# Eight start places modulo 128 bytes for the operands of a kernel's MLP products

## The chip, the core and the metric

The kernel runs on one core of a Trainium2 chip. A core has a matrix engine (TensorE, PE in the profile, with its loads of stationary operands shown apart as PEld), VectorE (DVE), ScalarE (ACT), GpSimd (POOL), and a queue that issues transfers (SyncE, SP). They work on tiles in an on-chip memory of 128 partitions; results of TensorE land in a second memory, PSUM. A tile takes the same bytes in every partition, so the place of an operand is one byte address, counted from the start of a partition.

The metric is the device time of one execution in microseconds (us), lower is better.

## The reference, cut to what matters

Two layers of a streaming encoder over 512 tokens of width 1024, in float32. A layer has a mixing part (a projection, pooling, differential attention, gated linear attention, an output projection) and an MLP; the change is in the MLP:

```python
def reference(x, ...):
    h = x
    for l in range(DEPTH):                    # 2
        u = rms_norm(h, norm1_g[l])
        ...                                   # the mixing part
        h = h + (mix @ w_out[l])
        z = rms_norm(h, norm2_g[l])
        h = h + jnp.square(jax.nn.relu(z @ w_mlp1[l])) @ w_mlp2[l]
    return rms_norm(h, final_norm_g)
```

`w_mlp1` is 1024 x 4096 and `w_mlp2` is 4096 x 1024 in each layer.

## The kernel before, in words

**Products in three.** Activations are kept transposed: a tile holds 128 features in the partitions and the 512 tokens along them. Each float32 operand is split into a high part in the type float32r and the float32r rest (`split`, L113 on: ScalarE casts the high part, L116; VectorE subtracts it, L117). A product is then three matmuls that add into one PSUM tile: high x high, high x low, low x high (`mm3`, L134 to L136, and `prod`, L904 to L906). The profile writes a matmul as out<-moving,stationary. The moving operand (activations, 512 or 256 columns) streams; the stationary operand (128 columns of weights) is loaded before it. For each matmul the trace has one load and one matmul.

**The first product of the MLP.** The 4096 features of the hidden layer are 32 output tiles of 128; two of them are a pair u, and four pairs are a quarter q, so there are 16 pairs in four quarters per layer. Pairs 0 and 1 of a layer are computed plainly (`plain`). The other 14 are computed by seven smaller products instead of eight (`seven`, a Strassen-like scheme over two halves of the input features and two halves of the tokens). The weights of a pair come in by DMA as raw1 and raw2; `prepare` makes four operands of them, each as a high and a low tile: a (tiles wh, wl), b, c and d (tiles bh, bl, ch, cl, dh, dl). On the moving side are the activations z (tiles zh, zl) and four sums of them, t1 to t4 (tiles th, tl), made once a layer (`sums_of_inputs`, `keep`). Each of the seven products is 12 matmuls of 256 columns:

| product, as the trace names it | moving | stationary |
|---|---|---|
| psx<-zh,wh | z | a |
| psz<-th,bh | t1 | b |
| psx<-th,ch | t2 | c |
| psy<-zh,dh | z | d |
| psz<-zh,ch | z | c |
| psx<-th,bh | t3 | b |
| psx<-th,wh | t4 | a |

That is 84 matmuls a pair, 28 pairs, 2352 matmuls.

**The second product.** The squared hidden tiles of a quarter are split into the tiles sh, sl (`acts`), which are the moving operand of the second product: for each of 8 output tiles m, one load of weights (`weights(wm2[l, q, m])`, tiles wh, wl), and 24 matmuls (8 tiles of the quarter x 3) into a PSUM tile psm (`second`). That is 1488 matmuls of 512 columns; the last two output tiles of the last quarter of layer 1 are done in token halves, which are 96 matmuls of 256 columns.

**Order.** TensorE's order in the MLP is that of the code. VectorE and ScalarE prepare the next pair's operands while TensorE works on this one (`prepare(u + 1)` stands behind `seven(u)`), so one pair's operands are ready ahead.

**Places.** A tile's address is given out by its pool when the program is built. All tiles named here begin at a multiple of 32 bytes. In the built program, modulo 128 bytes, zh, zl, wh and wl begin at 32, and th, tl, sh, sl and the b, c and d tiles begin at 96. Slices inside a tile step by multiples of 512 bytes, so they begin at the same place modulo 128 as their tile. Two places of the mixing part are read below: the tile y of the output projection (attention heads 2 and 3) begins at 0, and in the scores of the even heads the keys (kh, kl) begin at 0 and the queries (sq_) at 96.

Of the kernel before, what the change touches and what calls it, by code (L numbers as in the profile page):

```python
# [8 lines left out]
F32 = mybir.dt.float32  # L9
F32R = mybir.dt.float32r  # L10
# [23 lines left out]
PLAIN = 2  # L34
HT = T // 2
W = 16 + T
BIG = 1.0e30

LEAD = [(0, 0), (1, 0), (2, 0), (3, 0), (0, 1), (1, 1), (2, 1), (3, 1), (4, 0), (5, 0), (6, 0), (7, 0), (4, 1), (5, 1), (6, 1), (7, 1)]
# [30 lines left out]
def trunk(ctx: ExitStack, tc: tile.TileContext, xt, wfm, wdv, wgv, wout, wm1, wm2, poolw, wg2, par, con, msk, out, outt):  # L70
# [12 lines left out]
    def load(src, n=1024):  # L83
        raw = wp.tile([P, 1024], F32, name="raw", bufs=2)[:, 0:n]
        nc.sync.dma_start(out=raw, in_=src)
        return raw
# [33 lines left out]
            nc.vector.scalar_tensor_tensor(out=dst_l, in0=src, scalar=scale, in1=dst_h.bitcast(F32),  # L120
                                           op0=ALU.mult, op1=ALU.subtract)

    def cut(raw):
        n = raw.shape[1]
        wh = wp.tile([P, 1024], F32R, name="wh")[:, 0:n]
        wl = wp.tile([P, 1024], F32R, name="wl")[:, 0:n]
        split(wh, wl, raw)
        return wh, wl

    def weights(src, n=1024):  # L130
        return cut(load(src, n))

    def mm3(ps, sh, sl, mh, ml, first, last):
        nc.tensor.matmul(ps, sh, mh, start=first, stop=False)  # L134
# [98 lines left out]
    for l in range(L):  # L233
# [5 lines left out]
        for k in range(KT):  # L239
            for i, m, a, b in LOADS if l == 0 else ():  # L240
                if i == k:
                    if a == 0:
                        lead.append([wp.tile([P, 1024], F32R, name=n) for n in ("wh", "wl")])
                    split(lead[m][0][:, a:b], lead[m][1][:, a:b], first[m][:, a:b])
            split(uh[k], ul[k], h[k], g1[k])
        if l == 0:
# [558 lines left out]
        with ExitStack() as ph:  # L805
# [4 lines left out]
            sp = fast.enter_context(tc.tile_pool(name=f"sp{l}", bufs=1))  # L810
            acts, tz = {}, {}

            def plain(u, j):

                raw = wp.tile([P, 1024], F32, name="raw", bufs=2)
                nc.sync.dma_start(out=raw[:, 0:512], in_=wm1[l, u, j][:, 0:512])
                nc.sync.dma_start(out=raw[:, 512:1024], in_=wm1[l, u, 1 - j][:, 512:1024])
                wh, wl = cut(raw)
                ps = pm.tile([P, T], F32, name="psm", tag="pm")
                for k in range(KT):  # L820
                    s = slice(k * P, (k + 1) * P)
                    mm3(ps, wh[:, s], wl[:, s], zh[k], zl[k], k == 0, k == KT - 1)
                rl = mp.tile([P, T], F32, name="rl", bufs=3)
                nc.scalar.activation(rl, ps, AF.Relu)

                def rest():
                    nc.scalar.activation(rl, rl, AF.Square)
                    split(acts[u][0][:, j], acts[u][1][:, j], rl)

                return rest  # L830

            def sums_of_inputs():

                z = []

                def scaled_inputs(i):
                    zi = mp.tile([P, 2, T], F32R, name="z", tag=f"{'shsl'[2 * (i % 2):2 * (i % 2) + 2]}{2 + i // 2}", bufs=1).bitcast(F32)
                    for j in range(2):
                        nc.scalar.activation(zi[:, j], h[2 * i + j], AF.Copy, scale=g2[2 * i + j])
                    z.append(zi)  # L840

                def new(name):
                    return mp.tile([P, 4, HT], F32, name=name, tag="o4")

                def keep(i, t):
                    tz[i] = [sp.tile([P, 4, HT], F32R, name=f"t{n}{i}") for n in "hl"]
                    split(*tz[i], t)

                two = (slice(0, 2), slice(2, 4))
                t1 = new("t1")  # L850
                for i in range(2):
                    scaled_inputs(i)
                    nc.vector.tensor_sub(t1[:, two[i]], z[i][:, :, 0:HT], z[i][:, :, HT:T])
                keep(1, t1)
                t2 = new("t2")
                for i in range(2):
                    scaled_inputs(2 + i)
                    nc.vector.scalar_tensor_tensor(out=t2[:, two[i]], in0=t1[:, two[i]], scalar=-1.0, in1=z[2 + i][:, :, HT:T],
                                                   op0=ALU.mult, op1=ALU.subtract)
                keep(2, t2)  # L860
                yield
                t4 = new("t4")
                for i in range(2):
                    nc.vector.scalar_tensor_tensor(out=t4[:, two[i]], in0=t2[:, two[i]], scalar=-1.0, in1=z[2 + i][:, :, 0:HT],
                                                   op0=ALU.mult, op1=ALU.subtract)
                t3 = new("t3")
                for i in range(2):
                    nc.vector.tensor_sub(t3[:, two[i]], z[2 + i][:, :, HT:T], z[i][:, :, HT:T])
                keep(3, t3)
                keep(4, t4)  # L870

            def prepare(u):

                raw1 = load(wm1[l, u, 0])
                raw2 = sp.tile([P, 1024], F32, name="raw2", bufs=2)
                nc.sync.dma_start(out=raw2, in_=wm1[l, u, 1])
                a = cut(raw1)
                s13 = sp.tile([P, 2, 512], F32, name="s13")
                nc.vector.tensor_tensor(out=s13, in0=raw1.rearrange("p (a b) -> p a b", a=2),  # L879
                                        in1=raw2[:, 0:512].unsqueeze(1).broadcast_to([P, 2, 512]), op=ALU.add)  # L880
                b = [sp.tile([P, 2, 512], F32R, name=f"b{n}", bufs=2) for n in "hl"]
                split(*b, s13)
                s24 = sp.tile([P, 2, 512], F32, name="s24")
                nc.vector.tensor_add(s24[:, 0], s13[:, 1], raw1[:, 0:512])
                nc.vector.tensor_add(s24[:, 1], s24[:, 0], raw2[:, 512:1024])
                c = [sp.tile([P, 2, 512], F32R, name=f"c{n}") for n in "hl"]
                split(*c, s24)
                d = [sp.tile([P, 512], F32R, name=f"d{n}", bufs=2) for n in "hl"]
                split(*d, raw2[:, 512:1024])
                return a, b, c, d  # L890

# [65 lines left out]
            for q in range(QT):  # L957
                for u in range(q * UQ, (q + 1) * UQ):
                    if u == 0:
                        for i in range(PLAIN):  # L960
                            acts[i] = [mp.tile([P, 2, T], F32R, name=f"s{n}{i}", bufs=1) for n in "hl"]
                        left = [plain(0, 0)]
                        dg = token_norm(acc, True)[1]
                        left.append(plain(0, 1))
                        r2 = across(dg)
                        acc = sm.tile([P, T], F32, name="acc", bufs=1)
                        sums = sums_of_inputs()
                        next(sums)
                        left.append(plain(1, 0))
                        w = prepare(PLAIN)  # L970
                        left.pop(0)()
                        left.append(plain(1, 1))
                        list(sums)
                        for f in left:
                            f()
                    if u < PLAIN:
                        continue
                    acts[u] = [mp.tile([P, 2, T], F32R, name=f"s{n}{u % UQ}", bufs=1) for n in "hl"]
                    final = u % UQ == UQ - 1
                    old = late  # L980
                    late = seven(u, w, old, final)
                    if not final:
                        w = prepare(u + 1)
                    if old:
                        old[1]()
# [19 lines left out]
                every = slice(0, T)  # L1005
                lead = []
                for m in range(2):
                    w2t = weights(wm2[l, q, m])
                    ps = pm.tile([P, T], F32, name="psm", tag="pm")
                    second(ps, w2t, range(KT - 2), every)  # L1010
                    lead.append((ps, w2t))
                ends = l == L - 1 and q == QT - 1
                for m in range(KT - 2 if ends else KT):
                    if m < 2:
                        ps = lead[m][0]
                        second(*lead[m], range(KT - 2, KT), every)
                    else:
                        w2t = weights(wm2[l, q, m])
                        ps = pm.tile([P, T], F32, name="psm", tag="pm")
                        second(ps, w2t, range(KT), every)  # L1020
                    update(m, ps, every)
                    if q == QT - 1:
                        square_acc(acc, h[m], m == 0)
                    elif m == 2:
                        w = prepare((q + 1) * UQ)
                byhand.close()
                if ends:
                    w2t = [weights(wm2[l, q, m]) for m in range(KT - 2, KT)]
                    ph.enter_context(tc.manual_schedule(engines={mybir.EngineType.DVE}))
                    for half in range(2):  # L1030
                        n = slice(half * HT, (half + 1) * HT)
# [90 lines left out]
```

## Time and profile before

| | before |
|---|---|
| median of 2 runs | 1107.13 us (1106.85 to 1107.41) |
| the profiled execution | 1107.54 us, of which the trace's span is 1105.7 us |
| PE busy | 1090.8 us (99%), 6454 matmuls |
| DVE, ACT busy | 746.7 us (68%), 577.6 us (52%) |
| granted TensorE clock | 0.998 over the span |

Busy time of PE is the sum of intervals that overlap: matmuls are pipelined, and the next one starts before the one ahead has ended. How fast a row of matmuls goes is therefore read from the starts: the start of a later one less the start of an earlier one, divided by the number of matmuls between. This is called the pace below.

### The profile page before, as it was taken

How to read it: one execution, taken by the hardware profiler on the slowest of the kernel's cores; microseconds unless marked ns; L12 is line 12 of the kernel's file. 1: busy time of each engine (PE TensorE's matmuls, PEld its weight loads, DVE VectorE, ACT ScalarE, POOL GpSimd, SP SyncE). 2: the span in 40 equal slices, each digit the busy share in tenths (PEclk: the TensorE clock that was granted, in tenths of full speed). 3: DMA queues.
4: the chain of work that ended last, by engine and by line, in shares of the span. 5: the costliest groups of instructions: out<-in, count | busy, mean ns of one | idle time of the engine just before them, and what ended most of it. 6: DMA issues, size and time to landing. Idle time of an engine off the chain costs nothing.

```text
span 1105.7 us, 16213 instructions
## 1 busy us (share of the span) xinstructions
PE 1090.8 (99%) x6454; PEld 960.3 (87%) x6454; DVE 746.7 (68%) x1115; ACT 577.6 (52%) x998; POOL 47.4 (4%) x84
## 2 busy tenths in 40 slices
PE   7999999999999999999999999999999999999997
PEld 5888898888898898898887988888989989989986
DVE  5577774896676676675647588749766666666654
ACT  5526774685265264265434377748633733733742
POOL 2101000000000000000021100000000000000000
PEclk9999999999999999999999999999999999999999
DMA  6222211433322322312322131214232332332222
GB/s 210 86 65 71 77 58 57 146 104 108 120 96 88 122 97 84 124 60 68 103 61 84 59 95 58 79 56 152 96 115 86 106 115 81 111 114 79 75 76 76
DMA packets 32223, 102.75 MB, mean 93 GB/s; under 512 B 3698, under 2 KB 5524, under 8 KB 32148
## 3 DMA queue, kind: packets, MB, share of 16 engines
q1 hardware_dynamic: 31716, 101.17, 28.5%
q8 instruction: 50, 0.82, 0.3%
q10 hardware_dynamic: 432, 0.55, 0.1%
q14 instruction: 25, 0.20, 0.1%
HBM read 99.61 MB, written 2.10 MB: 92 GB/s over the span
## 4 chain that ended last, share of the span: by engine, by line
PE 97%; issue 1%; ACT 1%; DVE 1%; DMA 0%; SPq 0%; POOLq 0%; POOL 0%; DVEq 0%
PE psm L136 18%; PE psm L135 18%; PE psm L134 18%; PE psx L904 5%; PE psx L906 5%; PE psx L905 5%; PE psz L906 2%; PE psz L904 2%; PE psz L905 2%; PE psm L340 2%; PE psm L341 2%; PE psm L342 2%; PE po L483 1%; PE psy L904 1%; PE psy L906 1%; PE psy L905 1%
## 5 line engine op out<-in xcount | busy, mean ns | idle before, releaser
L116 ACT CAST wh<-raw 128x1024 fp32r<-128x1024 f32 (+2 forms) x155 | 160.0, 1034 | 293.9 <-PE psm L135 213.0
L117 DVE TENSOR_TENSOR wl<-raw,wh 128x1024 fp32r<-128x1024 f32 (+2 forms) x155 | 185.9, 1202 | 74.3 <-ACT wh L116 74.0
L136 PE MATMUL psm<-sh,wl 128*128 128x512 f32 (+1 forms) x528 | 204.5, 387 | 0.0
L135 PE MATMUL psm<-sl,wh 128*128 128x512 f32 (+1 forms) x528 | 203.3, 385 | 0.0
L134 PE MATMUL psm<-sh,wh 128*128 128x512 f32 (+1 forms) x528 | 201.5, 382 | 0.0
L1002 DVE TENSOR_TENSOR tm<-psm,rb 128x512 f32<-128x512 f32 (+1 forms) x66 | 44.5, 674 | 113.2 <-PE psm L136 113.2
L135 PEld LDWEIGHTS psm<-sl,wh 128*128 128x128 f32 x528 | 99.1, 188 | 21.5
L134 PEld LDWEIGHTS psm<-sh,wh 128*128 128x128 f32 x528 | 99.1, 188 | 20.6
L136 PEld LDWEIGHTS psm<-sh,wl 128*128 128x128 f32 x528 | 99.3, 188 | 18.5
L134 PE MATMUL psm<-uh,wh 128*128 128x512 f32 x224 | 95.7, 427 | 5.9 <-ACT uh L119 5.9
L135 PE MATMUL psm<-ul,wh 128*128 128x512 f32 x224 | 89.7, 400 | 0.5 <-DVE ul L120 0.5
L136 PE MATMUL psm<-uh,wl 128*128 128x512 f32 x224 | 89.5, 399 | 0.1
L134 PEld LDWEIGHTS psm<-uh,wh 128*128 128x128 f32 x224 | 43.1, 192 | 15.7 <-ACT uh L119 7.3
L340 PE MATMUL psm<-wh,uh 128*128 128x256 f32 (+1 forms) x192 | 56.6, 295 | 0.0
L342 PE MATMUL psm<-wh,ul 128*128 128x256 f32 (+1 forms) x192 | 54.7, 285 | 0.0
L341 PE MATMUL psm<-wl,uh 128*128 128x256 f32 (+1 forms) x192 | 54.6, 284 | 0.0
L135 PEld LDWEIGHTS psm<-ul,wh 128*128 128x128 f32 x224 | 43.1, 192 | 10.4 <-DVE ul L120 2.3
L136 PEld LDWEIGHTS psm<-uh,wl 128*128 128x128 f32 x224 | 43.0, 192 | 10.4 <-DVE wl L117 1.0
L453 ACT ACTIVATE pp<-psc,mn,nrt 128x128 f32<-128x128 f32 (+3 forms) x64 | 39.0, 615 | 13.9 <-DVE mn L450 12.0
L1003 DVE TENSOR_TENSOR h<-h,tm 128x512 f32<-128x512 f32 (+1 forms) x66 | 44.5, 674 | 1.5
L117 DVE TENSOR_TENSOR sl<-o,sh 128x1024 fp32r<-128x1024 f32 (+1 forms) x36 | 35.0, 987 | 11.2 <-ACT sh L116 11.2
L879 DVE TENSOR_TENSOR s<-raw,raw 128x1024 f32<-128x1024 f32 x28 | 34.2, 1221 | 6.4 <-DMA raw<-in_wm 6.4
(379 smaller groups left out, 2719.4 us busy)
## 6 DMA issues: line engine op xcount, KB each, us to landing
raw<-in_wm SPq DMA_DIRECT2D x120, 512.0 KB, 3.6
raw<-in_wfm SPq DMA_DIRECT2D x27, 512.0 KB, 3.6
raw<-in_wout SPq DMA_DIRECT2D x16, 512.0 KB, 3.6
raw<-in_wdv SPq DMA_DIRECT2D x8, 512.0 KB, 3.5
raw<-in_wm SPq DMA_DIRECT2D x16, 256.0 KB, 3.2
h<-in_xt SPq DMA_DIRECT2D x8, 256.0 KB, 6.2
raw<-in_wgv SPq DMA_DIRECT2D x4, 408.0 KB, 3.4
out<-o SPq DMA_DIRECT2D x8, 128.0 KB, 1.8
```

Source lines behind the costliest of these rows:

```text
L116: nc.scalar.copy(out=dst_h, in_=src)
L117: nc.vector.tensor_sub(dst_l, src, dst_h.bitcast(F32))
L134: nc.tensor.matmul(ps, sh, mh, start=first, stop=False)
L135: nc.tensor.matmul(ps, sh, ml, start=False, stop=False)
L136: nc.tensor.matmul(ps, sl, mh, start=False, stop=last)
L340: nc.tensor.matmul(ps, uh[k][:, ts], wh[:, s], start=k == 0, stop=False)
L341: nc.tensor.matmul(ps, uh[k][:, ts], wl[:, s], start=False, stop=False)
L342: nc.tensor.matmul(ps, ul[k][:, ts], wh[:, s], start=False, stop=k == KT - 1)
L904: nc.tensor.matmul(ps, sh[:, s], mh, start=first and k == 0, stop=False, skip_group_check=True)
L905: nc.tensor.matmul(ps, sh[:, s], ml, start=False, stop=False, skip_group_check=True)
L906: nc.tensor.matmul(ps, sl[:, s], mh, start=False, stop=k == 3, skip_group_check=True)
L1002: nc.vector.tensor_tensor(out=tm, in0=ps, in1=r2[:, n], op=ALU.mult)
```

## The change: what it does, and the diff

Tiles that hold operands of the MLP's products get 28 more floats (112 bytes) of room, and the operand begins at an offset inside the tile. The offsets are the eight entries of SPOT, in floats; in bytes they are 0, 32, 64, 96, 16, 48, 80, 112.

- The stationary operands a, b, c, d of pair u begin SPOT[u % 8] into their tiles.
- The stationary operands of the second product begin SPOT[m] into theirs, by output tile m.
- The moving operand of the second product, the tiles sh, sl of layer l and quarter q, begin SPOT[4 l + q] into theirs.
- The sums t1 to t4 begin 4 l floats into theirs: 0 bytes in layer 0, 16 in layer 1.
- The activations z and the weights of the plain pairs begin where they did.

The wider tiles shift the addresses of the tiles behind them; each tile still begins at the same place modulo 128 as before. The tiles now end at byte 229,072 of a partition, before at 224,992. The instructions of all five engines are the same, in the same order and with the same waits: only addresses differ, and no instruction is added or removed.

With "distance" for the start of the moving operand less the start of the stationary operand of the same matmul, modulo 128 bytes, the built programs have these numbers of matmuls:

| distance, bytes | 0 | 16 | 32 | 48 | 64 | 80 | 96 | 112 |
|---|---|---|---|---|---|---|---|---|
| seven products, before | 1344 | 0 | 0 | 0 | 1008 | 0 | 0 | 0 |
| seven products, after | 276 | 300 | 276 | 324 | 276 | 324 | 276 | 300 |
| second product (512 columns), before | 0 | 0 | 0 | 0 | 1488 | 0 | 0 | 0 |
| second product (512 columns), after | 192 | 192 | 192 | 192 | 168 | 192 | 168 | 192 |
| second product (256 columns), before | 0 | 0 | 0 | 0 | 96 | 0 | 0 | 0 |
| second product (256 columns), after | 0 | 0 | 0 | 0 | 48 | 0 | 48 | 0 |

The diff, cut to its core:

```diff
+PAD = 28
+SPOT = (0, 8, 16, 24, 4, 12, 20, 28)
...
-    def cut(raw):
+    def cut(raw, at=0):
         n = raw.shape[1]
-        wh = wp.tile([P, 1024], F32R, name="wh")[:, 0:n]
-        wl = wp.tile([P, 1024], F32R, name="wl")[:, 0:n]
+        wh = wp.tile([P, 1024 + PAD], F32R, name="wh")[:, at:at + n]
+        wl = wp.tile([P, 1024 + PAD], F32R, name="wl")[:, at:at + n]
...
-    def weights(src, n=1024):
-        return cut(load(src, n))
+    def weights(src, n=1024, at=0):
+        return cut(load(src, n), at)
...
+            def place(u):
+
+                at = SPOT[4 * l + u // UQ]
+                return [mp.tile([P, 2 * T + PAD], F32R, name=f"s{n}{u % UQ}", bufs=1)[:, at:at + 2 * T].rearrange("p (j n) -> p j n", j=2)
+                        for n in "hl"]
...
-                    tz[i] = [sp.tile([P, 4, HT], F32R, name=f"t{n}{i}") for n in "hl"]
+                    tz[i] = [sp.tile([P, 4 * HT + PAD], F32R, name=f"t{n}{i}")[:, 4 * l:4 * l + 4 * HT].rearrange("p (k n) -> p k n", k=4) for n in "hl"]
...
-                a = cut(raw1)
+                at = SPOT[u % 8]
+                a = cut(raw1, at)
...
-                b = [sp.tile([P, 2, 512], F32R, name=f"b{n}", bufs=2) for n in "hl"]
+                b = [sp.tile([P, 1024 + PAD], F32R, name=f"b{n}", bufs=2)[:, at:at + 1024].rearrange("p (a n) -> p a n", a=2) for n in "hl"]
...
-                    acts[u] = [mp.tile([P, 2, T], F32R, name=f"s{n}{u % UQ}", bufs=1) for n in "hl"]
+                    acts[u] = place(u)
...
-                    w2t = weights(wm2[l, q, m])
+                    w2t = weights(wm2[l, q, m], at=SPOT[m])
```

The tiles of c and d get the same treatment as those of b.

## Rows read from the trace of the kernel before

**Rows 1.** The page: busy time by engine, the granted clock, the chain.

```profile
span 1105.7 us, 16213 instructions
...
PE 1090.8 (99%) x6454; PEld 960.3 (87%) x6454; DVE 746.7 (68%) x1115; ACT 577.6 (52%) x998; POOL 47.4 (4%) x84
...
PEclk9999999999999999999999999999999999999999
...
PE 97%; issue 1%; ACT 1%; DVE 1%; DMA 0%; SPq 0%; POOLq 0%; POOL 0%; DVEq 0%
```

**Rows 2.** Waits, whole span: who waited for whom, us in total, times, longest.

```profile
ACT wh L116 <- PE psm L135: 213.0, 70, 6.2
...
DVE tm L1002 <- PE psm L136: 113.2, 47, 5.1
```

**Rows 3.** Groups by shape: count, busy us, mean ns, idle before.

```profile
L136 PE MATMUL psm<-sh,wl 128*128 128x512 f32 x496 | 195.4, 394 | 0.0
...
L904 PE MATMUL psx<-th,ch 128*128 128x256 f32 x112 | 31.7, 283 | 0.0
...
L904 PE MATMUL psx<-th,wh 128*128 128x256 f32 x112 | 30.9, 276 | 0.0
```

**Rows 4.** Timeline, PE, one round of seven products: start us, duration us, instruction.

```profile
480.72 0.28 PE L904 MATMUL psx<-th,wh 128*128 128x256 f32 x1
...
482.08 0.28 PE L904 MATMUL psx<-th,ch 128*128 128x256 f32 x1
...
483.52 0.29 PE L904 MATMUL psy<-zh,dh 128*128 128x256 f32 x1
...
484.90 0.28 PE L904 MATMUL psz<-zh,ch 128*128 128x256 f32 x1
...
486.26 0.28 PE L904 MATMUL psx<-th,bh 128*128 128x256 f32 x1
...
487.68 0.28 PE L904 MATMUL psx<-zh,wh 128*128 128x256 f32 x1
...
489.10 0.28 PE L904 MATMUL psz<-th,bh 128*128 128x256 f32 x1
...
490.53 0.28 PE L904 MATMUL psx<-th,wh 128*128 128x256 f32 x1
```

**Rows 5.** Timeline, PE, second product: the first of 24 matmuls, and of the next.

```profile
435.76 0.39 PE L134 MATMUL psm<-sh,wh 128*128 128x512 f32 x1
...
441.25 0.39 PE L134 MATMUL psm<-sh,wh 128*128 128x512 f32 x1
```

**Rows 6.** Timeline, PE, a plain product: matmuls 1, 13, 22 and 24 of 24.

```profile
215.40 0.39 PE L134 MATMUL psm<-zh,wh 128*128 128x512 f32 x1
...
218.16 0.39 PE L134 MATMUL psm<-zh,wh 128*128 128x512 f32 x1
...
220.20 0.39 PE L134 MATMUL psm<-zh,wh 128*128 128x512 f32 x1
...
220.65 0.39 PE L136 MATMUL psm<-zh,wl 128*128 128x512 f32 x1
```

**Rows 7.** Timeline, PE, output projection: six matmuls, and the next one.

```profile
187.25 0.39 PE L134 MATMUL psm<-y,wh 128*128 128x512 f32 x1
...
188.65 0.40 PE L134 MATMUL psx<-y,wxA 128*128 128x512 f32 x1
```

**Rows 8.** Timeline, PE, attention scores: the second of four matmuls, and the next product.

```profile
134.69 0.28 PE L446 MATMUL psc<-kl,sq__1084 128*128 128x256 f32 x1
...
135.04 0.39 PE L134 MATMUL psm<-uh,wh 128*128 128x512 f32 x1
```

**Rows 9.** Busy us (instructions) of PE, PEld, DVE, ACT, POOL, 480 to 490.

```profile
480.00:490.00 10.00, 10.00 (x88) 10.00 (x87) 8.57 (x12) 7.77 (x12) 0.00 (x0) 1.00 0.18 55
```

**Rows 10.** Groups by shape, DVE: count, busy us, mean ns, idle before.

```profile
L117 DVE TENSOR_TENSOR wl<-raw,wh 128x1024 fp32r<-128x1024 f32 x147 | 179.1, 1220 | 64.7 <-ACT wh L116 64.4
...
L1003 DVE TENSOR_TENSOR h<-h,tm 128x512 f32<-128x512 f32 x62 | 42.8, 690 | 1.4
...
L117 DVE TENSOR_TENSOR sl<-o,sh 128x1024 fp32r<-128x1024 f32 x20 | 24.5, 1226 | 5.7 <-ACT sh L116 5.7
...
L117 DVE TENSOR_TENSOR dl<-raw,dh 128x512 fp32r<-128x512 f32 x28 | 19.2, 686 | 0.3
...
L536 DVE TENSOR_TENSOR pl<-pl 128x512 f32<-128x512 f32 x8 | 5.5, 689 | 0.3
```

More of the change, by code (lines that the diff above doesn't have):

```diff
@@ L242, in trunk @@
                     if a == 0:
-                        lead.append([wp.tile([P, 1024], F32R, name=n) for n in ("wh", "wl")])
+                        lead.append([wp.tile([P, 1024 + PAD], F32R, name=n)[:, 0:1024] for n in ("wh", "wl")])
                     split(lead[m][0][:, a:b], lead[m][1][:, a:b], first[m][:, a:b])
@@ L836, in scaled_inputs @@
                 def scaled_inputs(i):
-                    zi = mp.tile([P, 2, T], F32R, name="z", tag=f"{'shsl'[2 * (i % 2):2 * (i % 2) + 2]}{2 + i // 2}", bufs=1).bitcast(F32)
+                    zi = mp.tile([P, 2 * T + PAD], F32R, name="z", tag=f"{'shsl'[2 * (i % 2):2 * (i % 2) + 2]}{2 + i // 2}",
+                                 bufs=1)[:, 0:2 * T].bitcast(F32).rearrange("p (j n) -> p j n", j=2)
                     for j in range(2):
@@ L885, in prepare @@
                 nc.vector.tensor_add(s24[:, 1], s24[:, 0], raw2[:, 512:1024])
-                c = [sp.tile([P, 2, 512], F32R, name=f"c{n}") for n in "hl"]
+                c = [sp.tile([P, 1024 + PAD], F32R, name=f"c{n}")[:, at:at + 1024].rearrange("p (a n) -> p a n", a=2) for n in "hl"]
                 split(*c, s24)
-                d = [sp.tile([P, 512], F32R, name=f"d{n}", bufs=2) for n in "hl"]
+                d = [sp.tile([P, 512 + PAD], F32R, name=f"d{n}", bufs=2)[:, at:at + 512] for n in "hl"]
                 split(*d, raw2[:, 512:1024])
@@ L960, in trunk @@
                         for i in range(PLAIN):
-                            acts[i] = [mp.tile([P, 2, T], F32R, name=f"s{n}{i}", bufs=1) for n in "hl"]
+                            acts[i] = place(i)
                         left = [plain(0, 0)]
@@ L1017, in trunk @@
                     else:
-                        w2t = weights(wm2[l, q, m])
+                        w2t = weights(wm2[l, q, m], at=SPOT[m])
                         ps = pm.tile([P, T], F32, name="psm", tag="pm")
@@ L1027, in trunk @@
                 if ends:
-                    w2t = [weights(wm2[l, q, m]) for m in range(KT - 2, KT)]
+                    w2t = [weights(wm2[l, q, m], at=SPOT[m]) for m in range(KT - 2, KT)]
                     ph.enter_context(tc.manual_schedule(engines={mybir.EngineType.DVE}))
```

## The prediction

> **What bounds the kernel now.** I read the page first. TensorE is busy 99% of the span, its clock is full in every slice, and the chain that ended last is PE for 97% [rows 1]. So only two things move the time: how fast TensorE gets through its matmuls, and whether somebody makes it wait. The view of waits, next, shows the feeders waiting for TensorE and not the other way round: ScalarE's casts of weights waited 213 us for buffers that TensorE still read, VectorE's updates 113 us for sums [rows 2]. In the groups by shape PE has no idle time ahead of the matmuls of the MLP, and products of the same size differ there: 283 ns a matmul for psx<-th,ch, 276 for psx<-th,wh [rows 3]. Busy times overlap, so I took the pace from starts in the timeline.
>
> One round of the seven products shows it [rows 4]. From one first matmul to the next, divided by 12:
>
> - distance 0 (moving and stationary operand begin at the same place modulo 128): psx<-th,ch 1.44 us, 120.0 ns a matmul; psx<-th,bh and psx<-zh,wh 1.42 us, 118.3; psz<-th,bh 1.43 us, 119.2. Mean 119.0 ns.
> - distance 64: psx<-th,wh and psz<-zh,ch 1.36 us, 113.3 ns; psy<-zh,dh 1.38 us, 115.0. Mean 113.9 ns.
>
> All are 256 columns, in one stretch, at one clock, behind one another on one engine. What goes with the difference is the distance: z at distance 0 (zh,wh) is slow and at 64 (zh,ch) fast, th with b and c is slow and with a fast. So I take it that the stream of a matmul and the load of stationary columns beside it get in each other's way, and that the distance sets how much. That is a reading, and its test is this change.
>
> With 512 columns the pattern is another: the second product, at distance 64, has 24 matmuls in 5.49 us, 228.8 ns [rows 5]; a plain product, at distance 0, 228.3 over the whole and 2.04 us / 9 = 226.7 where it is settled [rows 6]; the output projection from tile y, at distance 96, six in 1.40 us, 233.3 ns [rows 7].
>
> **The change, part by part.** Nothing is added, removed or reordered on any engine, and no transfer is changed. What changes is the distance of 2352 + 1488 + 96 matmuls, and the start of what VectorE and ScalarE write and read there.
>
> *Seven products.* Before, 1344 matmuls at distance 0 and 1008 at 64: 1344 x 119.0 + 1008 x 113.9 = 274.7 us. After, 276 at 0, 276 at 64, 1800 at six other distances. For those six no row of this product exists. Bounds: 113.3 ns, the fastest product of the round, and 120.0 ns, the slowest [rows 4]. The nearest rows are scores of 256 columns at distance 32, three matmuls in 0.35 us, 116.7 ns [rows 8]; that lies by the middle of 119.0 and 113.9, 116.45, and I take the middle. After: 276 x 119.0 + 276 x 113.9 + 1800 x 116.45 = 273.9 us. The term is -0.9 us. With both ends it is from 2352 x 113.3 = 266.5 us (-8.3) to 2352 x 120.0 = 282.2 us (+7.5).
>
> *Second product, 512 columns.* Before, 1488 x 228.75 = 340.4 us. After, 192 at distance 0 (228.3), 168 at 64 (228.75), 360 at 32 and 96, for which I take 233.3 from the y rows though y is another tile, and 768 at odd multiples of 16, for which no row stands. I take the mean of the four known distances, (228.3 + 228.75 + 233.3 + 233.3) / 4 = 230.9. Sum 343.6 us, +3.2 us. Ends: all at 226.7, -3.1 us; all at 233.3, +6.8 us.
>
> *Second product, 256 columns.* 48 of 96 go from distance 64 to 96: 48 x 2.55 ns = +0.1 us.
>
> *VectorE and ScalarE.* I cost their edits at nothing. Their instructions are the same; TensorE covers them, and in the fullest 10 us of a round VectorE is busy 8.57 and ScalarE 7.77 [rows 9]. That reads began elsewhere is seen already: L536 reads one tile at two starts that are 4 to 32 bytes apart, 689 ns for 512 columns, against 690 for the plain L1003 [rows 10]. Writes at a 16-byte start have no row; without the cover this is the rival with VectorE below.
>
> **Sum.** -0.9 + 3.2 + 0.1 = +2.4 us on the profiled execution's 1107.54 us. The median of the runs, 1107.13, lies 0.4 below that, so the forecast is 1109.5 us. With all ends at once it is from 1107.1 - 11.4 = 1095.7 to 1107.1 + 14.3 = 1121.4.
>
> Two per cent, about what a measurement of this kernel can tell from no change, is 22 us. The whole range of the pace lies inside it.
>
> **Rivals.**
>
> *Only equal places collide.* Then the six new distances are as good as 64, and the seven products keep 119.0 for 276 matmuls alone: 276 x 119.0 + 2076 x 113.9 = 269.3 us, -5.4. The second product has no place to gain, since it stood at 64, and stays. Time 1101.7. For it: the two paces of rows 4 are clearly apart, and most products there sit on the slow one. Against it: the y rows at distance 96 are slower than those at both 0 and 64. Chance 0.22.
>
> *Only 64 is clear (slower).* The load and the stream share something that repeats in 128 bytes, and every start but the opposite one meets it. In the seven products 2076 x 119.0 + 276 x 113.9 = 278.5 us, +3.7; in the second product 1320 matmuls go to 233.3, +6.0; the 96 give +0.2. Time 1117.0. It decides as soon as distances 16 and 48 pay what 0 pays with 256 columns, and what 96 pays with 512. For it: 64 was where 1488 + 1008 matmuls already stood, so most matmuls have more to lose than to win; rows 7. Against: the scores at distance 32, 116.7, are not at 119. Chance 0.18.
>
> *Places count for nothing.* What differs between the products of rows 4 would then be something that stays with the product, say the PSUM tile or its neighbours, and the time stays at 1107.1. Against it: psz at distance 0 is slow and psz at distance 64 fast, psx likewise, so the PSUM tile is not it. This is also what the Trainium skill would have: "SBUF — State Buffer", section "Who interferes with whom", gives TensorE two independent read ports, one for the moving operand and one for the loads, and says that it never waits on anyone. By that rule the 5.1 ns between the two groups of rows 4 would have another cause than the two operands' places, and the change would come to 0 instead of +2.4 us. Chance 0.13.
>
> *VectorE becomes the bound (slower).* If starts at 16 bytes make its writes longer, it is five instructions a pair, three of 1.22 us, one of 1.23 and one of 0.69 [rows 10] (b and c are of the size of wl), 5.6 us. It has 1.43 us to spare in 10 [rows 9], so this decides from 25% longer on. At half as long again it is 2.8 - 1.4 = 1.4 us a pair, x 28 = +39 us, 1146. The shifted reads of L536 speak against it. Chance 0.04.
>
> **How the numbers follow.** The forecast has 0.43. The range from 1100 to 1117 takes in the forecast's own width (1105 to 1114), the unchanged time, the rival of equal places but for its lower part (0.05), and the one with 64 clear up to its middle (0.09 left out); with VectorE's 0.04 some 0.18 is outside. Faster by over 2% would need more than every matmul at its best pace gives: 0.01. Slower by over 2% is the rival with VectorE: 0.04. Within 2%: 0.95.
>
> **What will show it.** In the timeline of the changed kernel the pace of a product should change from pair to pair with u % 8, and repeat where the distance repeats; distance 0 should be near 119 and 64 near 114 in whichever product they fall. That is right if psx<-th,ch, now at 120.0 in every pair, has fast pairs, and psz<-zh,ch slow ones. In the second product the pace should change with the output tile m. It is wrong if each product keeps its pace through all pairs. PE's share of the chain should stay at 97%, and DVE's mean of wl<-raw,wh at 1220 ns; if that rises, the rival with VectorE is at work. The forecast fails if the odd multiples of 16 are not like the mean of the others, since half of all matmuls stand there and nothing in this trace does.

## The result, and the profile after

The changed kernel took 1115.03 us (median of 2 runs, 1113.92 to 1116.13), against 1107.13 before: ratio 1.0072, 95% interval 1.0056 to 1.0088. It is slower by 0.7%, inside the range of the prediction, with no difference by the bound of 2%.

The page of the kernel after, the rows that answer to [rows 1]:

```profile
span 1114.3 us, 16213 instructions
...
PE 1099.5 (99%) x6454; PEld 963.7 (86%) x6454; DVE 747.0 (67%) x1115; ACT 576.3 (52%) x998; POOL 47.4 (4%) x84
...
PEclk9999999999999999999999999999999999999999
...
PE 97%; issue 1%; DVE 1%; DMA 0%; ACT 0%; SPq 0%; POOLq 0%; POOL 0%; DVEq 0%
```

TensorE is still the chain, and at the same granted clock. Its span grew by 8.6 us (1105.7 to 1114.3). No feeder became slow or late. In the views of the groups on VectorE, of the fullest stretch (PE, PEld, DVE, ACT, POOL) and of the waits, after:

```profile
L120 DVE TENSOR_TENSOR wl<-raw,wh 128x1024 fp32r<-128x1024 f32 x147 | 179.1, 1220 | 67.2 <-ACT wh L119 66.7
...
L120 DVE TENSOR_TENSOR dl<-raw,dh 128x512 fp32r<-128x512 f32 x28 | 19.2, 686 | 0.3
```

```profile
484.00:494.00 10.00, 10.00 (x87) 10.00 (x86) 8.51 (x12) 7.76 (x12) 0.00 (x0) 1.00 0.16 53
```

```profile
ACT wh L119 <- PE psm L138: 224.4, 73, 6.3
...
DVE tm L1013 <- PE psm L139: 117.8, 47, 5.2
```

The means, 1220 and 686 ns, are those of [rows 10], the fullness is that of [rows 9], and the feeders wait a little longer for TensorE than in [rows 2]. So the 8.6 us are in the pace of the matmuls. The same round as in [rows 4], from the timeline of PE after (start us, duration us, instruction):

```profile
484.04 0.28 PE L915 MATMUL psx<-th,wh 128*128 128x256 f32 x1
...
485.45 0.28 PE L915 MATMUL psx<-th,ch 128*128 128x256 f32 x1
...
486.87 0.28 PE L915 MATMUL psy<-zh,dh 128*128 128x256 f32 x1
...
488.28 0.28 PE L915 MATMUL psz<-zh,ch 128*128 128x256 f32 x1
...
489.70 0.28 PE L915 MATMUL psx<-th,bh 128*128 128x256 f32 x1
...
491.11 0.28 PE L915 MATMUL psx<-zh,wh 128*128 128x256 f32 x1
...
492.55 0.28 PE L915 MATMUL psz<-th,bh 128*128 128x256 f32 x1
...
493.98 0.28 PE L915 MATMUL psx<-th,wh 128*128 128x256 f32 x1
```

Seven products take 9.94 us instead of 9.81. The two paces of before, 1.36 to 1.38 and 1.42 to 1.44 us, are gone: all seven products stand at 1.41 to 1.44 us, those that were fast before included. The groups by shape say the same (count, busy us, mean ns): where [rows 3] had 283 for psx<-th,ch and 276 for psx<-th,wh, there is now one number.

```profile
L915 PE MATMUL psx<-th,ch 128*128 128x256 f32 x112 | 31.5, 281 | 0.0
...
L915 PE MATMUL psx<-th,wh 128*128 128x256 f32 x112 | 31.4, 281 | 0.0
```

The second product, its first matmul for output tiles 0 to 3 of one quarter, after:

```profile
428.20 0.39 PE L137 MATMUL psm<-sh,wh 128*128 128x512 f32 x1
...
433.72 0.40 PE L137 MATMUL psm<-sh,wh 128*128 128x512 f32 x1
...
439.28 0.39 PE L137 MATMUL psm<-sh,wh 128*128 128x512 f32 x1
...
444.88 0.40 PE L137 MATMUL psm<-sh,wh 128*128 128x512 f32 x1
```

5.52, 5.56 and 5.60 us for 24 matmuls, where [rows 5] had 5.49 for each. And a plain product, matmuls 13 and 22 of 24, as in [rows 6]:

```profile
218.61 0.39 PE L137 MATMUL psm<-zh,wh 128*128 128x512 f32 x1
...
220.69 0.39 PE L137 MATMUL psm<-zh,wh 128*128 128x512 f32 x1
```

2.08 us / 9 = 231.1 ns where before had 226.7, though neither z nor the plain weights were given another place modulo 128.

Summed from the starts over the whole trace, in us (ns a matmul):

| | before | after | |
|---|---|---|---|
| seven products, 2352 | 275.9 (117.3) | 278.6 (118.5) | +2.7 |
| second product, 1488 of 512 columns | 340.6 (228.9) | 344.6 (231.6) | +4.0 |
| second product, 96 of 256 columns | 12.1 | 12.2 | +0.1 |
| plain products, z with w, 192 | 44.7 (233.0) | 45.5 (237.2) | +0.8 |
| projections from u, 672 | 167.8 | 169.2 | +1.4 |
| all of TensorE | 1093.7 | 1102.3 | +8.6 |

### The profile page after: what moved, and what is told of

Read it like the earlier page. It is cut to its first block, busy times and chain, and to the rows that moved or that the text cites. A ratio compares the mean times of both kernels' runs of the same rounds, so it can differ in the third digit from the quotient of the medians.

```text
span 1114.3 us, 16213 instructions
## 1 busy us (share of the span) xinstructions
PE 1099.5 (99%) x6454; PEld 963.7 (86%) x6454; DVE 747.0 (67%) x1115; ACT 576.3 (52%) x998; POOL 47.4 (4%) x84
## 4 chain that ended last, share of the span: by engine, by line
PE 97%; issue 1%; DVE 1%; DMA 0%; ACT 0%; SPq 0%; POOLq 0%; POOL 0%; DVEq 0%
PE psm L139 18%; PE psm L138 18%; PE psm L137 18%; PE psx L915 5%; PE psx L916 5%; PE psx L917 5%; PE psz L915 2%; PE psz L916 2%; PE psz L917 2%; PE psm L343 2%; PE psm L344 2%; PE psm L345 2%; PE po L486 1%; PE psy L917 1%; PE psy L915 1%; PE psy L916 1%
## 5 line engine op out<-in xcount | busy, mean ns | idle before, releaser
L137 PE MATMUL psm<-sh,wh 128*128 128x512 f32 (+1 forms) x528 | 204.7, 388 | 0.0
L1013 DVE TENSOR_TENSOR tm<-psm,rb 128x512 f32<-128x512 f32 (+1 forms) x66 | 44.5, 674 | 117.9 <-PE psm L139 117.8
```

The source lines that it names most:

```text
L1013: nc.vector.tensor_tensor(out=tm, in0=ps, in1=r2[:, n], op=ALU.mult)
```

## The experiments

"Distance" is again the moving operand's start less the stationary one's, now also modulo 256 or 512 bytes; "pitch" is the step from the start of one tile to the start of the next. The distances are read from the addresses in the built programs, the paces from starts in the traces. Each kernel was timed in 5 rounds beside the kernel before (1105.5 to 1107.1 us). The paces are means over all matmuls of a kind, in ns:

| kernel | us | ratio to before | seven | second, 512 |
|---|---|---|---|---|
| E1 wider pitch, no offsets | 1115.74 | 1.0079 [1.0066, 1.0093] | 117.9 | 232.8 |
| E7 wider pitch, stationary tiles | 1113.33 | 1.0052 [1.0039, 1.0064] | 117.9 | 231.2 |
| E8 wider pitch, moving tiles | 1110.17 | 1.0027 [1.0018, 1.0037] | 117.6 | 230.4 |
| E6 pitch 4608 for s | 1107.26 | 0.9998 [0.9990, 1.0007] | 117.3 | 228.9 |
| E2 all at 64 modulo 128 | 1110.70 | 1.0033 [1.0020, 1.0045] | 117.7 | 229.0 |
| E3 all at 0 modulo 128 | 1117.34 | 1.0093 [1.0080, 1.0106] | 119.4 | 232.4 |
| E4 all at 32 modulo 128 | 1123.60 | 1.0152 [1.0139, 1.0165] | 118.6 | 234.3 |
| E5 64 or 448 modulo 512 | 1096.79 | 0.9908 [0.9893, 0.9923] | 114.0 | 228.9 |
| E9 192 or 320 modulo 512 | 1111.47 | 1.0046 [1.0034, 1.0058] | 117.6 | 229.0 |
| E12 as E5 modulo 256 only | 1096.47 | 0.9913 [0.9897, 0.9930] | 114.1 | 228.9 |
| E10 places at a regular pitch | 1112.31 | 1.0058 [1.0045, 1.0071] | 117.8 | 231.2 |
| E11 E5, second product at 0 | 1095.68 | 0.9914 [0.9900, 0.9927] | 114.3 | 226.8 |

**The pitch.** The change does two things: offsets, and tiles of 4224 bytes in place of 4096. E1 keeps the tiles and sets every offset to 0, so that every distance modulo 128 is that of before (the edit is against the changed kernel):

```diff
-SPOT = (0, 8, 16, 24, 4, 12, 20, 28)
+SPOT = (0,) * 8
...
-                    tz[i] = [sp.tile([P, 4 * HT + PAD], F32R, name=f"t{n}{i}")[:, 4 * l:4 * l + 4 * HT].rearrange("p (k n) -> p k n", k=4) for n in "hl"]
+                    tz[i] = [sp.tile([P, 4 * HT + PAD], F32R, name=f"t{n}{i}")[:, 0:4 * HT].rearrange("p (k n) -> p k n", k=4) for n in "hl"]
```

> The room of 112 bytes in the tiles stays, all eight offsets are 0. Every operand begins at the same place modulo 128 as before the change; only the pitch from tile to tile is 4224 instead of 4096 bytes. Theory 'distance' (the start of the moving operand less that of the stationary operand, modulo 128, sets the pace): time as before, 1107 us within 1, seven products 117 ns a matmul, second product 228.8. Theory 'pitch' (the pace depends on the addresses above 128 bytes as well, and 4096-byte pitches were a lucky regular pattern): most of the 7.9 us are here already, 1113 to 1116 us; seven products about 118.3, second product about 231.5, and the plain products at distance 0, which the change slowed from 228.3 to about 233 though neither operand has an offset, are slow here too. Theory 'changing places' (what costs is that the place changes from pair to pair and from output tile to output tile): as before, 1107.

1115.74 us: the wider tiles alone are enough for the whole slowdown, and the offsets on top of them changed nothing in the time that can be measured. They did move the parts: with offsets the second product has 231.6 ns instead of 232.8, the seven products 118.5 instead of 117.9. A tile of 4224 bytes is 4096 + 128, so the high and the low tile of an operand, and a tile and its successor, lie 128 bytes apart modulo 256, where before nearly all pitches were multiples of 512. In E1 the second product's distances are 64 and 192 modulo 256, mixed inside each output tile, and it went from 228.9 to 232.8 ns; before, all 1488 were at 64. Two output tiles in the timeline of PE of E1, where [rows 5] had 5.49 us:

```profile
442.88 0.39 PE L137 MATMUL psm<-sh,wh 128*128 128x512 f32 x1
...
448.47 0.39 PE L137 MATMUL psm<-sh,wh 128*128 128x512 f32 x1
...
454.05 0.39 PE L137 MATMUL psm<-sh,wh 128*128 128x512 f32 x1
```

5.59 and 5.58 us. A product whose moving tiles stayed at one place modulo 256 kept its pace in some rounds; from the same timeline:

```profile
486.26 0.28 PE L915 MATMUL psz<-zh,ch 128*128 128x256 f32 x1
...
487.62 0.28 PE L915 MATMUL psx<-th,bh 128*128 128x256 f32 x1
...
489.03 0.28 PE L915 MATMUL psx<-zh,wh 128*128 128x256 f32 x1
```

psz<-zh,ch takes 1.36 us, the next 1.41.

E6 gives s, and the float32 inputs of the sums that share its tiles, a pitch of 4608 bytes, which is wider still but a multiple of 512 (against the kernel before):

```diff
-                    acts[u] = [mp.tile([P, 2, T], F32R, name=f"s{n}{u % UQ}", bufs=1) for n in "hl"]
+                    acts[u] = [mp.tile([P, 2 * T + 128], F32R, name=f"s{n}{u % UQ}", bufs=1)[:, 0:2 * T].rearrange("p (j n) -> p j n", j=2) for n in "hl"]
```

> Before, with the eight tiles sh, sl at a pitch of 4608 bytes, a multiple of 512 but not of 4096, and no offset; every distance modulo 512 is as before. Theory 'irregular pitch modulo 512': nothing changes, 1107, second product 228.9 ns. Theory 'any pitch other than 4096 costs': second product 231 to 233 ns, +3 to +6 us, 1110 to 1113.

1107.26 us with both paces as before: the width of these tiles is free, the odd multiple of 128 is not. E7 takes the 4224 bytes for the stationary tiles wh, wl, b, c, d alone, E8 for the moving tiles s and t alone (E1 with PAD left out of the others):

> e1_pad_only with the pitch of 4224 bytes on the stationary tiles alone (wh, wl, b, c, d); moving tiles at 4096. If the stationary side matters: plain products of the MLP slow as in e1 (237 against 233.0 ns in the mean), second product slow too, and most of e1's 8.7 us. If it were the moving side alone: plain and second product as before, 1107.

> e1_pad_only with the pitch of 4224 bytes on the moving tiles alone (sh, sl, th, tl); stationary tiles at 4096. The plain products and the projections have neither tile changed and must stay at 233.0 and 249.8 ns. If either side's pitch is enough (what counts is that high and low tiles stand at different distances): second product at 231 to 233 ns, +3 to +6 us, 1110 to 1113. If the stationary side alone matters: 1107.

+6.3 and +3.1 us, each against the kernel before timed beside it: neither side does it alone, and together, 9.4, they are about E1's +8.7.

**The distance.** E2, E3 and E4 leave offsets and pitches as before and shift whole groups of tiles by unused spacers. The one of E3, and one of four in E2:

```diff
+            mp.tile([P, 16], F32, name="gm", bufs=1)
...
+                    sp.tile([P, 16], F32, name="gb", bufs=1)
```

> Before, with spacers of 64 bytes between tiles, no tile widened: z, u begin at 96 and b, c, d at 32, so that all seven products, the second product and the projections stand at distance 64; all pitches stay 4096 or 2048. Theory 'distance': the 1344 matmuls of the seven products that stood at 0 go from 119.0 to 113.9 ns, -6.9 us, time about 1100. Theory 'pitch' alone, with the distance of no account: 1107 within 1, paces of the seven products as before, product by product.

> Before, with one spacer of 64 bytes ahead of the tiles of the MLP: t, s, b, c, d begin at 32 like z and the weights, so that the seven products and the second product stand at distance 0; pitches as before. Theory 'distance': 1008 matmuls go from 113.9 to 119.0, +5.1 us, the second product from 228.8 to 228.3, -0.7; time about 1111.5. Distance of no account: 1107 within 1.

> Before, with spacers: the weights, b, c, d begin at 0 and z, t, s at 32, so that all products of the MLP and the projections stand at distance 32; pitches as before. Theory 'distance' as the prediction priced it: seven products 116.45 ns, -0.9 us or a little more, second product and the projections 233.3, +6.8 and about +3; time about 1116. Distance of no account: 1107 within 1.

E2 missed: with every product at 64 modulo 128, the "good" distance, it was slower than before. psx<-th,wh slowed from 113.4 to 118.0 ns, psz<-zh,ch from 113.8 to 118.2. Its spacers had moved these from 64 and 448 modulo 512 to 192 and 320. E3 and E4 show the worst places: at 0 and 128 modulo 256 the seven products have 118.6 to 120.0, waits left out, and at 160 the second product has 234.3. Both missed as well, by 5.8 and 7.6 us: E3's second product, expected at distance 0 with 228.3 ns, stood at 128 modulo 256 and had 232.4, and E4's seven products had 118.6 ns where 116.45 was expected.

**The period.** E5 is E2 with two spacers made larger, so that all seven products are at 64 or 448 modulo 512:

```diff
             res.tile([P, 16], F32, name="gz", bufs=1)
-            res.tile([P, 16], F32, name="ge", bufs=1)
+            res.tile([P, 112], F32, name="ge", bufs=1)
...
-                sp.tile([P, 16], F32, name="gt", bufs=1)
+                sp.tile([P, 112], F32, name="gt", bufs=1)
```

> As e2_all64, with spacers that add up to 512 bytes, so that every product of the MLP stands 64 or 448 bytes apart (that is 64 either way) modulo 512, where e2 had 192 and 320 too. Theory 'distance modulo 512' (e2's psx<-t4,w went from 113.4 to 118.0 ns though it kept 64 modulo 128, because it went from 64 to 192 modulo 512): all seven products come near 113.4 to 115 ns, seven products 268 to 271 us instead of 275.9, time 1099 to 1102. Theory 'history' (a pace is carried on from the products ahead, so a distance alone does not set it): 117 to 118 ns as in e2, time 1107 to 1111.

1096.79 us, faster than both kernels. The same round in the timeline of PE of E5:

```profile
474.67 0.28 PE L911 MATMUL psx<-th,wh 128*128 128x256 f32 x1
...
476.03 0.28 PE L911 MATMUL psx<-th,ch 128*128 128x256 f32 x1
...
477.39 0.28 PE L911 MATMUL psy<-zh,dh 128*128 128x256 f32 x1
...
481.47 0.28 PE L911 MATMUL psx<-zh,wh 128*128 128x256 f32 x1
...
482.83 0.28 PE L911 MATMUL psz<-th,bh 128*128 128x256 f32 x1
```

1.36 us for each: psx<-th,ch, at 120.0 ns before, now has 113.3, and so have all seven in every pair but for waits. Those fall on psz<-zh,ch and psx<-th,bh in the 8 of the 28 pairs that end a quarter, where the order is another, and make the mean of 114.0 in the table. E9 puts all seven at 192 or 320 modulo 512 by other spacers:

> All pitches are as before; spacers put the operands of the seven products at a distance of 192 or 320 bytes modulo 512 (64 or 192 modulo 256, and 64 modulo 128), where the kernel with all of them at 64 or 448 modulo 512 took 1096.8 us. The second product stays at 64 modulo 512; the projections from u and the plain products go to 192. If only the distance modulo 256 counts, this is that kernel again: 113.3 ns in the seven products, 268 us, about 1097 us. If the distance modulo 512 counts, 192 and 320 are slow as the single products at these distances were in the kernel with all operands at 64 modulo 128 (117.9 to 118.2 ns): 2352 x 118 = 277.5 us for the seven, +1.6 us to before, with the plain products and projections 0 to +2 us: 1108 to 1111 us.

1111.47 us. That looked like a period of 512, but E9 had also turned signs modulo 256 (64 for 192 and the reverse) in five of the seven. E12 has the distances of E5 modulo 256 exactly, with five of the seven products 256 bytes off modulo 512 ("ge" and "gt" of 48 floats):

> Spacers as in the kernel with all operands of the seven products at 64 or 448 modulo 512 (1096.8 us), but two of them 256 bytes shorter, so that every distance in the MLP and of the projections from u is the same as there modulo 256, and five of the seven products (z with w, c and d, t3 with b, t4 with w) and the projections from u are 256 bytes off modulo 512 (192 and 320 in place of 448 and 64). The kernel before with 192 and 320 in these five (1111.5 us) had the opposite signs modulo 256, so it does not tell 256 from 512. If the pattern repeats every 256 bytes, this is the fast kernel again: 113.3 ns in all seven, 268 us, 1097 us. If it repeats every 512 bytes or more, the five go to about 117.8 ns: 1680 x 4.5 ns = +7.6 us, and the projections from u back to before (+2.7 us): 1104 to 1108 us.

1096.47 us; the timeline of PE of E12:

```profile
475.74 0.28 PE L911 MATMUL psx<-th,ch 128*128 128x256 f32 x1
...
477.10 0.28 PE L911 MATMUL psy<-zh,dh 128*128 128x256 f32 x1
...
478.46 0.28 PE L911 MATMUL psz<-zh,ch 128*128 128x256 f32 x1
...
479.82 0.28 PE L911 MATMUL psx<-th,bh 128*128 128x256 f32 x1
```

The pattern repeats every 256 bytes, then, and the period of 512 that E5 seemed to confirm falls. E2 and E9 say the same from the slow side: their places agree modulo 256 and not modulo 512, and six of the seven products have the same pace in both within 0.2 ns. What E9 lacks is another thing. In E5 and E12 all moving operands begin at one place modulo 256. In E2 and E9 those of t1 and t2 begin 128 bytes from the others. The timeline of PE of E9, one product in the first two pairs, at the same distance of 192:

```profile
240.11 0.28 PE L911 MATMUL psx<-zh,wh 128*128 128x256 f32 x1
...
241.48 0.28 PE L911 MATMUL psz<-th,bh 128*128 128x256 f32 x1
...
248.55 0.28 PE L911 MATMUL psx<-zh,wh 128*128 128x256 f32 x1
...
249.97 0.28 PE L911 MATMUL psz<-th,bh 128*128 128x256 f32 x1
```

1.37 us, and then 1.42. Another product of E9, psz<-zh,ch, has its operands at 224 and 160 modulo 256, where E5 has those of psx<-zh,wh (481.47 to 482.83, 1.36 us):

```profile
245.72 0.28 PE L911 MATMUL psz<-zh,ch 128*128 128x256 f32 x1
...
247.13 0.28 PE L911 MATMUL psx<-th,bh 128*128 128x256 f32 x1
```

1.41 us, 117.8 ns, at the places that gave 113.3. So a distance of 64 or 192 modulo 256 allows 113.3 ns, but does not give it: what runs around a product counts as well. E8 shows it too. It moved the tiles t and s alone; psz<-zh,ch kept both its operands' places modulo 512, and went from 113.2 to 115.2 ns by pair to 113.3 to 117.8. That it is what ran before fits the starts inside a product: in the kernel before, psy<-zh,dh at 483.52 us takes 121, 122 and 116 ns for its first three matmuls behind the slow psx<-th,ch, and 113 to 114 for the rest, all at one distance. That a step of 128 in the moving operand loses the fast pace fits E1, E2, E8, E9 and the changed kernel; it was not tried by itself. It is not the only way: in E7 no moving operand steps so, all distances of psx<-th,wh are 64 or 192 modulo 256, and it has 118.6 ns in the median pair.

**The places by themselves.** E10 gives the change's offsets to operand a and to the weights of the second product, at a pitch of 4608 bytes; all else is as before:

```diff
-        wh = wp.tile([P, 1024], F32R, name="wh")[:, 0:n]
+        wh = wp.tile([P, 1152], F32R, name="wh")[:, at:at + n]
...
-                a = cut(raw1)
+                a = cut(raw1, SPOT[u % 8])
...
-                    w2t = weights(wm2[l, q, m])
+                    w2t = weights(wm2[l, q, m], at=SPOT[m])
```

> The eight places of the change for operand a of the pairs and for the weights of the second product, but with wh and wl at a pitch of 4608 bytes, a multiple of 512, and every other tile as before. So all 24 matmuls of an output tile have one distance modulo 512: 64, 32, 0, 480, 48, 16, 496, 464 for m = 0 to 7. If the change's places cost nothing by themselves and only the pitch did, this is 1107.1 us, with the second product at 228.9 ns for every m. If the distance modulo 512 sets the pace of 512 columns too, the pace goes by m: near 227 to 229 at 0 and 64, and for the six others between 229 and 234; at their middle, 231.5, the second product gains 1110 x 2.6 ns = +2.9 us, and the two products with operand a go to between 113.4 and 120 (-1.5 to +2.7 us): 1108 to 1113 us.

1112.31 us. At a regular pitch the places do count. The timeline of PE, the second product's output tiles 1 to 3 and the start of the next:

```profile
430.37 0.39 PE L135 MATMUL psm<-sh,wh 128*128 128x512 f32 x1
...
435.96 0.39 PE L135 MATMUL psm<-sh,wh 128*128 128x512 f32 x1
...
441.40 0.39 PE L135 MATMUL psm<-sh,wh 128*128 128x512 f32 x1
...
447.00 0.39 PE L135 MATMUL psm<-sh,wh 128*128 128x512 f32 x1
```

5.59, 5.44 and 5.60 us, the same in every quarter within 0.01. In ns by distance modulo 256, with the transitions between tiles left out:

| | 0 | 16 | 32 | 48 | 64 | 208 | 224 | 240 |
|---|---|---|---|---|---|---|---|---|
| second product, 512 columns | 226.7 | 228.7 | 233.4 | 231.7 | 230.1 | 233.2 | 233.1 | 233.3 |
| psx<-th,wh, 256 columns | 120.0 | 119.3 | 117.0 | 117.1 | 113.3 | 117.7 | 118.2 | 118.1 |

Of the places tried here, narrow and wide matmuls want different ones: 64 is best and 0 worst with 256 columns, 0 is best with 512. (At 64 the kernel before had 228.9 with 512 columns, E10 has 230.1: here too the distance is not all.) It is the distance that goes with the pace, and not the place of the stationary tile: z and t4 meet the same tiles of a, and where a begins at 160 modulo 256, psx<-th,wh (distance 64) has 113.3 ns and psx<-zh,wh (distance 0) 119.3; where it begins at 224, they have 120.0 (distance 0) and 116.4 (distance 192). The second product came out at +3.5 us, the seven at +1.2; the projections from u, whose places are those of before, are 2.0 us shorter in this trace. The span of the profiled execution is longer by 2.9 us only, the median by 6.3: the execution profiled here, 1110.97 us, was the shortest of six, and the one profiled before, 1107.54, lies 1.5 us above the median of before in these rounds.

E11 joins the two: E5, with the weights of the second product 64 bytes into tiles of 4608, at distance 0:

> The kernel with all operands of the seven products at 64 or 448 modulo 512 (1096.8 us), and in addition wh and wl at a pitch of 4608 bytes, the weights of the second product 64 bytes into them, so that its 1488 wide matmuls go from a distance of 64 to 0 modulo 512. The kernel with the eight places at a regular pitch had 226.7 ns at distance 0 and 230.1 at 64 in this product; before had 228.9 at 64. If the distance modulo 512 sets the pace of wide matmuls as there, the second product goes from 340.6 to 1488 x 226.7 = 337.3 us, -3.3 us: 1093.5 us. If 0 was fast there only because of what stood around it, nothing changes: 1096.8 us. If 0 is slow with wide matmuls as it is with narrow ones (345.8 us in the kernel with all operands at 0 modulo 128, though its second product was at 128 modulo 512), +5 us: 1102 us.

The second product went from 340.6 to 337.5 us, as expected. The whole, 1095.68 us and 0.9914, can't be told from E5 and E12: in its trace the seven products gave back 0.6, the projections from u 0.8 and the 256-column part of the second product 0.5 us, and the sum over TensorE is 1.4 us less. Its page:

```profile
span 1091.9 us, 16213 instructions
...
PE 1077.6 (99%) x6454; PEld 949.2 (87%) x6454; DVE 747.0 (68%) x1115; ACT 577.0 (53%) x998; POOL 47.4 (4%) x84
```

## Why the prediction was right in its range and wrong in its sum

- **The range.** 1115.0 us lies inside the range of 1100 to 1117, but above the 1105 to 1114 that the prediction gave to its own sum. That the range held it is in part luck: it was drawn from the paces by distance, and the 8.7 us that E1 shows for the wider tiles had no place in it.
- **What bounds the kernel: right.** TensorE's pace is all that moved: +8.6 us in the sum over its starts, +8.6 in the span.
- **The distance sets the pace: right in kind, wrong in its period.** E5 takes psx<-th,ch from 120.0 to 113.3 ns with nothing but addresses, and E10 shows a pace by distance in one and the same product. But "the same place modulo 128" was the wrong measure. 64 and 448 modulo 512, which I called one distance, are 64 and 192 modulo 256, and 0 and 128, one distance to me as well, differ too: 0 gives 512 columns 226.7 ns, 128 gives 232.4 (E3). In the trace of before, products at 64 and at 192 both had the fast pace, and none of the MLP's stood at 128, so it could not show it. The 115.0 ns of psy<-zh,dh, which the prediction averaged into distance 64, are 113 to 114 behind a slow start of three matmuls; the sum has no term for what ran before.
- **The step that failed** is the count of what changes: "the distance of 2352 + 1488 + 96 matmuls". It counts offsets and prices the wider tiles at nothing. The tiles alone cost 8.7 us (E1). So the plain products, whose operands were given no offset, moved too (+0.8, as in E1 and E7), and have no term in the sum. The projections from u have none either; their +1.4 is not clearly the tiles', since with the same places E1 has -0.7, and their sum holds waits (165.8 to 168.2 us in E3, E6, E8 and E10, which leave them where they were). The offsets are not free either: part of them at a regular pitch costs 6.3 us (E10). The two do not add, so the 7.9 us can't be divided between them.
- **Seven products, -0.9 us predicted, +2.7 measured.** The middle pace I took for six distances, 116.45, was 118.0 to 118.6 (long waits left out), and the 113.9 of distance 64 was lost: after, 64 has 117.8 and 0 has 118.0. The sign I looked for, psx<-th,ch with fast pairs, is not there: its 12 matmuls took 1.439 to 1.440 us in every pair before and 1.402 to 1.461 after. psz<-zh,ch did turn slow: 1.359 to 1.382 before, over 1.41 in 26 of 28 pairs after. But with 64 and 0 alike after, the pace does not go by the distance modulo 128, as the sign had it.
- **Second product, +3.2 predicted, +4.0 measured, for a reason that holds in part.** It changes with the output tile, as foretold, and the mean of 230.9 was close to 231.6. But E1, which has no offsets, has 232.8, so the wider tiles alone give as much; at a regular pitch the same eight distances gave 231.2 (E10).
- **Rivals.** "Places count for nothing" falls with E5 and E10. The Trainium skill, in "SBUF — State Buffer", section "Who interferes with whom", has two independent read ports for TensorE and says that it never waits on anyone, which leaves places no way to count. The runs differ from that: one product has 113.3 and 120.0 ns at two distances (E10). Whether it is at the ports that the two operands meet, no run shows. "Only 64 is clear", 1117.0, is near the time, but not the cause: in E2 everything is at 64 modulo 128, and it is slow. "Only equal places collide" falls with E4, where no two operands of a product begin at the same place and each product has 116.75 ns or more. "VectorE becomes the bound" did not come: 1220 ns as before.
- The forecast, 1109.5, is 5.5 us short: 3.6 in the seven products, 0.8 in the second, 2.2 in products without a term, less 1.1 for the rest of the sum and for the run profiled.

## What to carry over

Where TensorE is the bound, widening a tile is a change of addresses for every tile behind it: pad to a multiple of the period (256 bytes here by the distances; the padded pitch that was run, 4608, is a multiple of 512), and price the shift as well as the offset. Compare starts per product, not means over the kernel: two products of one size with two paces, in one stretch, were the hint to 10 us (E5) that had nothing to do with the order of work. A distance rule read from one kernel holds for the period that the kernel happens to show; before resting a sum on it, look whether the trace holds pairs that would tell a longer period.

## What the runs showed of the hardware that was not expected

- The pace of float32r matmuls with a load for each depends on where the two operands begin, with a period of 256 bytes (E5 and E12, E2 and E9): 113.3 to 120.0 ns with 256 columns, 226.7 to 234.3 with 512. Over the kernel that is from 1095.7 us (E11) to 1123.6 (E4), 2.5%, at one granted clock.
- The best distance tried is another with 256 columns (64 or 192, 113.3 ns) than with 512 (0, 226.7 ns).
- The distance is not all: at the same places modulo 256 a product has 113.3 or 117.8 ns, by what runs around it (E5 and E9, E8). That it is what ran before is likely from the starts inside a product, but was not tried by itself; what brings the fast pace back stays open. So does what the load and the stream share; no run here looks inside.
